# Diagonal products of chunk pairs in one run, and the first chunks' skip term through the decay matrix

## The chip, the cores and the metric

The kernel runs on one core of a Trainium2 chip. The metric is the device time of one launch in microseconds (us), the median of several runs. The core has a matrix engine (TensorE, PE in the profile, with its weight loads as PEld), a vector engine (VectorE, DVE), a scalar engine (ScalarE, ACT), a general engine (GpSimd, POOL) and an engine that mostly issues transfers (SyncE, SP). Each engine runs its own instructions in the order in which they stand; between engines semaphores order the work.

## The reference, cut to what matters

One layer of a diffusion backbone on 512 latent tokens and 256 context tokens, width 1024, all in 32-bit floats: a combined input projection feeds a bidirectional state-space mixer (SSD) and a windowed attention; both are gated, merged and projected; a convolutional feed-forward block follows. The change lies in the SSD branch, which has 32 heads of 64 columns in 4 groups of 8 heads, and works in chunks of 128 tokens. Per direction it computes, with `cs` the running sum of the log decay within a chunk:

```python
decay_to_end = jnp.exp(cs[..., -1:] - cs)
states = jnp.einsum('bcsgn,bgrcs,bcsgrp->bcgrpn', bc, decay_to_end, xc)
...
cb = jnp.einsum('bclgn,bcsgn->bgcls', cc, bc)
scores = cb[:, :, None] * jnp.exp(segsum(ac))
y_diag = jnp.einsum('bgrcls,bcsgrp->bclgrp', scores, xc)
y_off = jnp.einsum('bclgn,bcgrpn,bgrcl->bclgrp', cc, states[:, :-1], jnp.exp(cs))
return (y_diag + y_off)...
...
y = yf + jnp.flip(yb, axis=1)
y = y + d_skip * xs          # the skip term, one factor a head
out = rmsnorm(y * silu(z), g)
```

`y_diag` is the diagonal product: within a chunk, a 128x128 decay matrix per head times that head's 64 columns of input. Forward and backward are folded into one decay matrix E per head, so that the main diagonal, on which both directions meet, and the skip term `d_skip * xs` need a correction that is diagonal as well.

## The kernel before, in words

The projections are large matrix products with 512 result columns, each as three passes over operands that are split into a high and a low half (`gemm`, L238 high by high, L239 low by high, L241 high by low). Their weights come by DMA, are cast by ACT (L183, `whi`), and the rest is taken by DVE (L184, `wlo`). A list of small steps is run between the k-steps of such a product, so that the SSD branch is laid between projection products and never stands alone.

`ssd_steps(g)` writes the SSD branch of group g. For each of 4 chunks there is `chunk_in(c)` and `chunk_out(c)`:

- `chunk_in` loads the decays (`fb`), multiplies C and B into `cb` on PE (L1696), takes its diagonal `cbd` on DVE (L1698), and makes on POOL 8 numbers per token, `coef` (L1577, L1574): the factor that the diagonal correction and the skip term put on `xs`. ACT and DVE build the two tiles E of 4 heads each (L1719, L1722, L1723, L1726); DVE multiplies them by `cb` (L1730). For chunks 1 to 3 POOL spreads `coef` on a diagonal (`dg`, two tiles) and adds it to E (two additions).
- `chunk_out` multiplies the forward state Sf and the backward state Sb[c] by C (L1754, 4 matmuls each; a matmul of 32-bit operands leaves two records in the trace); DVE weighs both by the decays (L1756, `te`). Then come the diagonal products E·xs (L1762): 8 matmuls of 64 columns, of which two neighbours use the two halves of the array. `advance` moves the forward state on (matmul L1597 from `xw` and `Bk`; POOL multiplies the state by its decay, DVE adds, L1600). POOL adds both `te` into `y`. `late`, run some steps later, adds the diagonal product to `y` (DVE, L1779) and multiplies by the gate `zs` (POOL; for chunk 3 DVE).

For chunk 0 the skip and the correction go another way: POOL makes `dx` = `xs`·`coef`, and `late` adds it to the diagonal product in PSUM by 4 transposes on PE (L1778).

The backward states Sb[2], Sb[1] and Sb[0] come from the steps `back(3)`, `back(2)` and `back(1)`, each an `advance` of its own. In groups 0 to 2 all three are written ahead of `chunk_in(0)`; in group 3 `back(2)` and `back(1)` are written behind it.

The small PSUM tiles (`mis`) rotate through 5 banks. A scheduler sets the order of instructions on each engine by its own due times, except that POOL's instructions of this branch, made by `gp` and `gs`, keep the order in which the program writes them:

```python
def gp(*a):
    return tc.keep_in_program_order(G.tensor_tensor(*a))
```

Line numbers are those of the kernel before. Up to L1703 they hold after the change too; behind it L1719, L1722, L1723, L1726 and L1730 become L1722, L1725, L1726, L1729 and L1733; L1754, L1756, L1762 and L1779 become L1756, L1758, L1768 and L1782.

Of the kernel before, what the change touches and what calls it, by code (L numbers as in the profile page):

```python
# [9 lines left out]
F32 = mybir.dt.float32  # L10
# [3 lines left out]
ALU = mybir.AluOpType  # L14
# [4 lines left out]
P = 128  # L19
# [25 lines left out]
def tile_hybrid_layer(  # L45
# [32 lines left out]
    V, S, G, T = nc.vector, nc.scalar, nc.gpsimd, nc.tensor  # L78
# [3 lines left out]
    hpool = ctx.enter_context(tc.tile_pool(name="hpool", bufs=1))  # L82
# [13 lines left out]
    def bank(name):  # L96
        pool, w = banks_[name]
        return pool.tile([P, 512 * w], F32, tag=name, name=name)
# [11 lines left out]
    def misb():  # L110
        return bank("mis")
# [32 lines left out]
    for j, t in enumerate((wdn[0], DSUMS[1], DSUMS[2], DSUMS[5], DSUMS[4], wdn[1], wdn[3])):  # L144
        for u in range(DU):
            n = min(2, DK - 2 * u) * HC
# [99 lines left out]
    ident = cpool.tile([P, P], F32, name="ident")  # L246
# [181 lines left out]
    with tc.tile_pool(name="spool", bufs=1) as sp:  # L428
# [237 lines left out]
        for j in range(KT):  # L666
# [46 lines left out]
            x = ("hi", "lo") if j >= NU else ("hh", "hl")  # L713
# [31 lines left out]
        for n in range(2):  # L745
            for j in range(KT):
                x = ("hi", "lo") if j >= NU else ("hh", "hl")
# [668 lines left out]
    zp = zpool.enter_context(tc.tile_pool(name="zpool", bufs=1, side="right", reuse_waits="tile"))  # L1416
    bp = bpool.enter_context(tc.tile_pool(name="bpool", bufs=1, reuse_waits="tile"))
# [18 lines left out]
    def h8(a):  # L1436
        return a.rearrange("p (h d) -> p h d", h=8)

    def bc64(a):
        return a.unsqueeze(2).to_broadcast([P, 8, 64])  # L1440
# [132 lines left out]
    def gp(*a):  # L1573
        return tc.keep_in_program_order(G.tensor_tensor(*a))  # L1574
# [4 lines left out]
    def ssd_steps(g):  # L1579
        d = GR[g]  # L1580
# [84 lines left out]
        def far_in(c, g=g):  # L1665

            far = bp.tile([P, 2, 4, P], F32, tag="far", name="far", bufs=2)
            for u in range(2):
                a = bass.AP(
                    tensor=us_d.tensor, offset=us_d[c, u, 0, g].offset, ap=[[0, 64], [16 * P, 2], [1, 512]]  # L1670
                )
                dma = nc.sync.dma_start(far[64 * u : 64 * u + 64].rearrange("p r j t -> p r (j t)"), a)
                if not g and not c:
                    tc.add_manual_dep(dma.ins, M_LOADS["x", 16].ins.name, QUEUED, reason="decays behind a projection's weights")
            GR[g]["far", c] = far

        def chunk_in(c):

            if not g and not c:
                far_in(0)  # L1680
            fb = []
            for dr in range(2):
                f = bp.tile([P, 8, P], F32, tag="fb", name="fb", bufs=4)
                a = bass.AP(
                    tensor=cs_d.tensor, offset=cs_d.offset + (32 * dr + 8 * g) * L + c * P, ap=[[0, P], [L, 8], [1, P]]
                )
                dma = nc.sync.dma_start(f, a)
                if not g and not c:
                    tc.add_manual_dep(dma.ins, M_LOADS["x", 16].ins.name, QUEUED, reason="decays behind a projection's weights")
                fb.append(f)  # L1690
            d["E"] = []

            def products():
                cb = d["cb"] = misb()
                tok = slice(c * P, (c + 1) * P)
                T.matmul(cb[:, :P], d["BT"][:, tok], d["CT"][:, tok], start=True, stop=True)  # L1696
                cbd = bp.tile([P, 1], F32, tag="cbd", name="cbd", bufs=2)
                V.tensor_tensor_reduce(  # L1698
                    cb[:, P : 2 * P], cb[:, :P], ident, op0=ALU.mult, op1=ALU.add, scale=1.0, scalar=0.0, accum_out=cbd
                )  # L1700
                coef = d["coef"] = bp.tile([P, 8], F32, tag="coef", name="coef", bufs=2)
                gs(coef, TT[:, c, 8 * g : 8 * g + 8], cbd, None, ALU.mult)
                gp(coef, coef, bcs[:, 8 * g : 8 * g + 8], ALU.add)  # L1703
                d["dg"] = [diagonal(q) for q in range(2)] if c else None

            def diagonal(q):
                dg = bp.tile([P, 4, P], F32, tag="dg", name="dg", bufs=2)
                w = d["coef"][:, 4 * q : 4 * q + 4].unsqueeze(2).to_broadcast([P, 4, P])
                gp(dg, ident.unsqueeze(1).to_broadcast([P, 4, P]), w, ALU.mult)
                return dg  # L1710

            def decays():
                for q in range(2):
                    E = bp.tile([P, 4, P], F32, tag="E", name="E", bufs=3)
                    eb = misb()
                    F4 = fb[0][:, 4 * q : 4 * q + 4, :]
                    for u in range(4):
                        h = 8 * g + 4 * q + u
                        e0 = S.activation(E[:, u, :], F4[:, u, :], AF.Identity, bias=TX[:, c, 0, h : h + 1])  # L1719
                        if u == 0 and c:  # L1720
                            tc.keep_in_program_order(e0)
                        S.activation(eb[:, u * P : (u + 1) * P], fb[1][:, 4 * q + u, :], AF.Identity, bias=TX[:, c, 1, h : h + 1])  # L1722
                    V.copy_predicated(E, sel.unsqueeze(1).to_broadcast([P, 4, P]), eb.rearrange("p (h l) -> p h l", h=4))  # L1723
                    d["E"].append(E)
                for E in d["E"]:  # L1725
                    S.activation(flat(E), flat(E), AF.Exp)  # L1726

            def weighed():
                for q, E in enumerate(d["E"]):  # L1729
                    V.tensor_tensor(E, E, d["cb"][:, :P].unsqueeze(1).to_broadcast([P, 4, P]), ALU.mult)  # L1730
                    if c:
                        gp(E, E, d["dg"][q], ALU.add)

            if g in BY_BLOCKS and not c:
                decays()
                BETWEEN[1:2] = [lambda f=BETWEEN[1]: (f(), products(), weighed())]
            else:
                products()
                decays()
                weighed()  # L1740
            if g and c > 1:
                square()
            if g < 3 and c == 3:
                far_in(0, g + 1)

        def chunk_out(c):
            xs, E, far = d["xs"], d["E"], d.pop(("far", c))
            tok = slice(c * P, (c + 1) * P)
            parts = []
            for dr, s in ((0, d["Sf"]), (1, d["Sb"][c])):  # L1750
                ps = misb()
                for ct in range(4):
                    z = slice(ct * P, (ct + 1) * P)
                    T.matmul(ps[:, z], s[:, z], d["CT"][:, tok], start=True, stop=True)  # L1754
                t = tmp("te")
                V.tensor_tensor(t, ps, flat(far[:, dr]), ALU.mult)  # L1756
                parts.append(t)

            yd = misb()
            for h in range(8):  # L1760
                o = yd[64 * (h % 2) : 64 * (h % 2) + 64, (h // 2) * P : (h // 2 + 1) * P]
                T.matmul(o, xs[:, c, h * 64 : (h + 1) * 64], E[h // 4][:, h % 4, :], start=h < 2, stop=c > 0 and h > 5)  # L1762
            dx = None
            if not c:
                dx = zp.tile([P, 512], F32, tag="th", name="dx", bufs=1)
                gp(h8(dx), h8(xs[:, c, :]), bc64(d["coef"]), ALU.mult)
            if c < 3:
                d["Sf"] = advance(d["Sf"], 0, c, weigh_in(0, c))  # L1768
            y = bp.tile([P, 512], F32, tag="tf", name="y", bufs=1)
            gp(y, parts[0], parts[1], ALU.add)  # L1770

            def late():

                if c < 3:
                    far_in(c + 1)
                for ct in range(0 if c else 4):
                    z = slice(ct * P, (ct + 1) * P)
                    tc.keep_in_program_order(T.matmul(yd[:, z], dx[:, z], ident, start=False, stop=ct == 3, is_transpose=True))  # L1778
                tc.keep_in_program_order(V.tensor_tensor(y, yd, y, ALU.add))  # L1779
                z = d["zt"][:, :, tok]  # L1780
                x = y.rearrange("p (a t) -> p a t", a=4)
                if c == 3:  # L1782
                    V.tensor_tensor(z, x, z, ALU.mult)
                else:
                    gp(z, x, z, ALU.mult)
                if g and c in (0, 3):
                    square()

            assert not BETWEEN
            if g < 3:  # L1790
                BETWEEN.extend([lambda: None] * 4 + [lambda: (late(), turn(1)), turn])
            else:
                BETWEEN.extend([lambda: None] * 2 + [late])
# [116 lines left out]
    q2 = hpool.tile([P, L], F32, name="q2")  # L1910
# [535 lines left out]
```

## Time and profile before

| | |
|---|---|
| median of 3 runs | 1215.3 us (1214.98 to 1215.76) |
| the profiled execution's own time | 1215.35 us |
| its span in the trace | 1213.6 us, TensorE clock granted 0.999 |
| busy | PE 1203.6 us, PEld 1005.6, DVE 918.6, ACT 684.4, POOL 263.8 |
| the SSD stage with its projections, 429 to 712 us of the span | PE 282.65 us busy of 283.00 |

The span is 1.75 us shorter than the execution's time; the rest lies around it. A PE record of the trace covers a matmul from its start to its end, and neighbours overlap, so what a matmul costs is the step from its start to the start of the next, not its length. PE is busy nearly throughout, so a row of PE starts is a clock for the whole kernel: what makes PE start later makes the kernel end later, if nothing behind it absorbs it.

### The profile page before, as it was taken

To read this page: it belongs to the slowest core of one execution; us is meant where nothing else is said; L and a number is where in the kernel's file an instruction comes from. 1 tells how busy PE (TensorE), PEld (TensorE's weight loads), DVE (VectorE), ACT (ScalarE), POOL (GpSimd) and SP (SyncE) were. 2 spreads that over 40 slices of the span, in tenths; PEclk is the share of its full clock that TensorE was granted. 3 is DMA by queue.
4 is the path that set the end of the run, shared out by engine and by line. 5 is a ranking of instruction groups with operands and counts; after the bars stand their busy time and mean duration, and the time that the engine had idled before them with its cause. 6 is when DMAs were issued, how large, how long until landed. Compare 5 with 4: busy or idle time off the path is not lost.

```text
span 1213.6 us, 17847 instructions
## 1 busy us (share of the span) xinstructions
PE 1203.6 (99%) x6429; PEld 1005.6 (83%) x6429; DVE 918.6 (76%) x1476; ACT 684.4 (56%) x1269; POOL 263.8 (22%) x274
## 2 busy tenths in 40 slices
PE   9999999999999999999999999999999999999998
PEld 6798888888878878788787887888988888888886
DVE  4857887888565588788887978677677767668787
ACT  4557887778543467476575664223544343436654
POOL 0000121100102546264382762000200100110021
PEclk9999999999999999999999999999999999999999
DMA  9655889844747737566477668687266634437662
GB/s 367 253 148 185 161 229 271 170 133 139 170 140 240 228 113 199 157 162 192 145 178 264 176 228 265 221 251 242 50 163 148 195 117 138 130 107 226 213 185 97
DMA packets 129417, 224.30 MB, mean 185 GB/s; under 512 B 27336, under 2 KB 70640, under 8 KB 129328
## 3 DMA queue, kind: packets, MB, share of 16 engines
q1 hardware_dynamic: 115248, 195.61, 52.0%
q0 software_dynamic: 13792, 27.27, 10.1%
q8 instruction: 51, 0.84, 0.3%
q14 instruction: 38, 0.31, 0.1%
q10 hardware_dynamic: 288, 0.27, 0.1%
HBM read 196.17 MB, written 45.02 MB: 199 GB/s over the span
## 4 chain that ended last, share of the span: by engine, by line
PE 90%; DMA 3%; DVE 2%; POOL 2%; issue 1%; ACT 1%; SPq 0%; DVEq 0%; POOLq 0%; ACTq 0%
PE acc L241 18%; PE acc L238 18%; PE acc L239 18%; PE score L979 3%; PE po L1028 3%; PE pt L1015 2%; PE mis L582 2%; PE mis L1754 2%; PE mis L1597 2%; PE mis L2304 2%; PE mis L2302 2%; PE mis L2303 2%; DMA xs_d<-xb 1%; PE acc L2304 1%; PE acc L2302 1%
## 5 line engine op out<-in xcount | busy, mean ns | idle before, releaser
L184 DVE TENSOR_TENSOR wlo<-wraw,whi 128x1024 fp32r<-128x1024 f32 (+1 forms) x115 | 148.3, 1289 | 89.2 <-ACT whi L183 88.3
L183 ACT CAST whi<-wraw 128x1024 fp32r<-128x1024 f32 (+1 forms) x115 | 120.2, 1046 | 154.2 <-PE acc L239 103.4
L238 PE MATMUL acc<-hlh,whi 128*128 128x512 f32 x472 | 192.8, 409 | 0.0
L241 PE MATMUL acc<-hlh,wlo 128*128 128x512 f32 x472 | 185.6, 393 | 0.0
L239 PE MATMUL acc<-hll,whi 128*128 128x512 f32 x472 | 185.0, 392 | 0.0
L238 PE MATMUL acc<-mh,whi 128*128 128x512 f32 x368 | 143.3, 389 | 0.0
L239 PE MATMUL acc<-ml,whi 128*128 128x512 f32 x368 | 143.2, 389 | 0.0
L241 PE MATMUL acc<-mh,wlo 128*128 128x512 f32 x368 | 143.2, 389 | 0.0
L241 PEld LDWEIGHTS acc<-hlh,wlo 128*128 128x128 f32 x472 | 88.6, 188 | 19.9 <-issue 0.5
L238 PEld LDWEIGHTS acc<-hlh,whi 128*128 128x128 f32 x472 | 88.8, 188 | 17.6 <-issue 2.8
L239 PEld LDWEIGHTS acc<-hll,whi 128*128 128x128 f32 x472 | 88.9, 188 | 17.4 <-issue 2.2
L238 PEld LDWEIGHTS acc<-mh,whi 128*128 128x128 f32 x368 | 69.1, 188 | 14.4
L241 PEld LDWEIGHTS acc<-mh,wlo 128*128 128x128 f32 x368 | 69.1, 188 | 14.3
L239 PEld LDWEIGHTS acc<-ml,whi 128*128 128x128 f32 x368 | 69.1, 188 | 14.2
L164 POOL DMA_DIRECT2D dsum<-wdn x24 | 25.3, 1118 | 194.3 <-DVE wlo L1112 183.7
L988 DVE CUSTOM_DVE_ANT_0 p<-score,winm,nsink 128x512 f32<-128x512 f32 (+1 forms) x64 | 51.8, 810 | 15.3 <-PE score L979 13.8
L995 ACT ACTIVATE p<-p,mneg 128x512 f32<-128x512 f32 (+1 forms) x64 | 49.7, 777 | 15.4 <-DVE mneg L988 14.9
L813 DVE SCALAR_TENSOR_TENSOR tm<-wraw,csil,tm 128x512 f32<-128x512 f32 x56 | 45.9, 819 | 13.1 <-DMA wraw<-wm 12.4
L1023 DVE TENSOR_TENSOR ptl<-pt,pth 128x512 fp32r<-128x512 f32 x72 | 47.5, 685 | 8.4 <-ACT pth L1019 7.7
L238 PE MATMUL acc<-hch,whi 128*128 128x256 f32 x176 | 53.2, 302 | 0.0
L1112 DVE TENSOR_TENSOR wlo<-wraw,whi 128x1024 fp32r<-128x1024 f32 x30 | 36.7, 1223 | 18.3 <-ACT whi L1109 18.2
L241 PE MATMUL acc<-hch,wlo 128*128 128x256 f32 x176 | 49.8, 283 | 0.0
(458 smaller groups left out, 3054.3 us busy)
## 6 DMA issues: line engine op xcount, KB each, us to landing
wraw<-wup SPq DMA_DIRECT2D x44, 512.0 KB, 4.0
dsum<-wdn POOLq DMA_DIRECT2D x24, 704.0 KB, 8.7
wraw<-wm SPq DMA_DIRECT2D x32, 512.0 KB, 4.1
fb<-cs_d SPq DMA_DIRECT2D x32, 512.0 KB, 7.5
wraw<-wx SPq DMA_DIRECT2D x24, 512.0 KB, 4.1
wm<-wm SPq DMA_DIRECT2D x16, 512.0 KB, 7.9
wraw<-wz SPq DMA_DIRECT2D x16, 512.0 KB, 4.7
far<-us_d SPq DMA_DIRECT2D x32, 256.0 KB, 5.1
```

Of the source, the lines that this page charges most:

```text
L183: F["cast"] = S.copy(hi[:, :n], r[:, :n])
L184: F["sub"] = V.tensor_tensor(lo[:, :n], r[:, :n], raw(hi[:, :n]), ALU.subtract)
L238: T.matmul(ps, wh, xh[:, k0 + k, :], start=a, stop=False)
L239: T.matmul(ps, wh, xl[:, k0 + k, :], start=False, stop=False)
L241: T.matmul(ps, wl, xh[:, k0 + k, :], start=False, stop=b)
L813: V.scalar_tensor_tensor(acc, r[:, u * 512 : u * 512 + 512], sc, acc, ALU.mult, ALU.add)
L988: V.tensor_tensor_reduce(p[:, :w], d["ps"][i][:, o0 : o0 + w], m, op0=ALU.add, op1=ALU.min, scale=1.0, scalar=nsink[:, h : h + 1], accum_o ...
L995: S.activation(p, p, AF.Exp, bias=d["mneg"][:, i : i + 1], scale=-1.0, accum_out=d["den"][:, i : i + 1])
L1023: V.tensor_tensor(d["ptl"][x], d["pt"][x], raw(d["pth"][x]), ALU.subtract)
L1112: sum_step(V.tensor_tensor(d["w"][1], d["r"], raw(d["w"][0]), ALU.subtract), 1 + (4 <= g < 12))
L2302: T.matmul(ps, h, wh, start=st, stop=False, skip_group_check=True)
L2304: T.matmul(ps, h, wl, start=False, stop=en, skip_group_check=True)
```

## The change

- Chunk 0's skip and correction term goes into the decay matrix as in the other chunks: POOL makes two `dg` and two additions to E, in place of one `dx`; the 4 transposes L1778 are gone.
- The diagonal products of chunk 0, and in groups 0 to 2 of chunk 2, are held back and run right before those of the next chunk: one run of 16 matmuls, into two PSUM banks, where there were two runs of 8. In group 3 chunks 2 and 3 keep runs of their own. Of 16 runs 9 are left.
- So that E of both chunks can live together, an odd chunk's second E tile has a buffer of another pool (`rbc4`), and a held chunk's `y` too (`q2`).
- `late` handles both chunks of a run: two additions L1782 on DVE in a row, and both gate multiplications.

```diff
@@ products
-                d["dg"] = [diagonal(q) for q in range(2)] if c else None
+                d["dg"] = [diagonal(q) for q in range(2)]
@@ decays
-                    E = bp.tile([P, 4, P], F32, tag="E", name="E", bufs=3)
+                    if c % 2 and q:
+                        E = hpool.tile([P, 4, P], F32, tag="rbc4", name="E")
+                    else:
+                        E = bp.tile([P, 4, P], F32, tag="E", name="E", bufs=3)
@@ weighed
-                    if c:
-                        gp(E, E, d["dg"][q], ALU.add)
+                    gp(E, E, d["dg"][q], ALU.add)
@@ chunk_out
-            yd = misb()
-            for h in range(8):
-                o = yd[64 * (h % 2) : 64 * (h % 2) + 64, (h // 2) * P : (h // 2 + 1) * P]
-                T.matmul(o, xs[:, c, h * 64 : (h + 1) * 64], E[h // 4][:, h % 4, :], start=h < 2, stop=c > 0 and h > 5)
-            dx = None
-            if not c:
-                dx = zp.tile([P, 512], F32, tag="th", name="dx", bufs=1)
-                gp(h8(dx), h8(xs[:, c, :]), bc64(d["coef"]), ALU.mult)
+            held = c == 0 or c == 2 and g < 3
+            d.setdefault("held", []).append((c, E))
+            done = []
+            for n, Es in [] if held else d.pop("held"):
+                yd = misb()
+                for h in range(8):
+                    o = yd[64 * (h % 2) : 64 * (h % 2) + 64, (h // 2) * P : (h // 2 + 1) * P]
+                    T.matmul(o, xs[:, n, h * 64 : (h + 1) * 64], Es[h // 4][:, h % 4, :], start=h < 2, stop=h > 5)
+                done.append((n, yd))
...
-            y = bp.tile([P, 512], F32, tag="tf", name="y", bufs=1)
+            y = hpool.tile([P, 512], F32, tag="q2", name="y") if held else bp.tile([P, 512], F32, tag="tf", name="y", bufs=1)
             gp(y, parts[0], parts[1], ALU.add)
+            d["y", c] = y
@@ late
-                for ct in range(0 if c else 4):
-                    z = slice(ct * P, (ct + 1) * P)
-                    tc.keep_in_program_order(T.matmul(yd[:, z], dx[:, z], ident, start=False, stop=ct == 3, is_transpose=True))
-                tc.keep_in_program_order(V.tensor_tensor(y, yd, y, ALU.add))
...
+                for n, yd in done:
+                    y = d.pop(("y", n))
+                    tc.keep_in_program_order(V.tensor_tensor(y, yd, y, ALU.add))
+                    z = d["zt"][:, :, n * P : (n + 1) * P]
...
```

How this moves instructions, at three places. In the rows a name is a tile of the program, out<-in, then the shape of an instruction and how many stand in a row; `-` marks rows of before, `+` rows of after. First, PE in group 0 at chunk 1, where the pair's products now run (`CT` is C, `st` a state, `xw` and `Bk` the operands of `advance`, `BT` is B):

```order
 L239 MATMUL acc<-hcl,whi 128x256
 L241 MATMUL acc<-hch,wlo 128x256
-L1754 MATMUL mis<-CT,st 128x128 x8
-L1762 MATMUL mis<-E,xs 64x128 x8
+L1756 MATMUL mis<-CT,st 128x128 x8
+L1768 MATMUL mis<-E,xs 64x128 x16
 L1597 MATMUL mis<-xw,Bk 128x512
 L1696 MATMUL mis<-CT,BT 128x128
```

The run has twice its matmuls; at chunk 0 the run L1762 is gone, and L1597 follows L1756 directly.

Second, POOL in group 3 from the first backward step on (`st<-st,eT` is the multiplication of an `advance`, the last one before `y` that of the forward state, the others those of `back(3)`, `back(2)` and `back(1)`):

```order
 L1574 TENSOR_TENSOR st<-st,eT 128x512
 L1577 TENSOR_SCALAR coef<-TT,cbd 128x8
 L1574 TENSOR_TENSOR coef<-coef,bcs 128x8
-L1574 TENSOR_TENSOR st<-st,eT 128x512 x2
-L1574 TENSOR_TENSOR dx<-xs,coef 128x512
-L1574 TENSOR_TENSOR st<-st,eT 128x512
+L1574 TENSOR_TENSOR dg<-ident,coef 128x512 x2
+L1574 TENSOR_TENSOR E<-E,dg 128x512 x2
+L1574 TENSOR_TENSOR st<-st,eT 128x512 x3
 L1574 TENSOR_TENSOR y<-te 128x512
```

The multiplications of `back(2)` and `back(1)` stood right behind `coef`; now two `dg` and two additions to E stand between. On DVE the addition L1600 of `back(2)` has moved behind the two multiplications of E by `cb`, where that of `back(1)` stood already; two `te` and a `wlo` still follow them.

Third, PE at the same place, chunk 0 of group 3:

```order
 L239 MATMUL acc<-hll,whi 128x512
 L241 MATMUL acc<-hlh,wlo 128x512
-L1754 MATMUL mis<-CT,st 128x128 x8
-L1762 MATMUL mis<-E,xs 64x128 x8
+L1756 MATMUL mis<-CT,st 128x128 x4
+L238 MATMUL acc<-hlh,whi 128x512
+L239 MATMUL acc<-hll,whi 128x512
+L241 MATMUL acc<-hlh,wlo 128x512
+L238 MATMUL acc<-hlh,whi 128x512
+L1756 MATMUL mis<-CT,st 128x128 x4
 L1597 MATMUL mis<-xw,Bk 128x512
 L1696 MATMUL mis<-CT,BT 128x128
```

The four products with the forward state stand where they stood; the four with the backward state Sb[0] have moved behind four matmuls of the projection, and the diagonal products have gone to chunk 1.

More of the change, by code (lines that the diff above doesn't have):

```diff
@@ L1775, in late @@
                     far_in(c + 1)
-                for ct in range(0 if c else 4):
-                    z = slice(ct * P, (ct + 1) * P)
[L1778 to L1785, printed above, removed]
+                for n, yd in done:
+                    y = d.pop(("y", n))
+                    tc.keep_in_program_order(V.tensor_tensor(y, yd, y, ALU.add))
+                    z = d["zt"][:, :, n * P : (n + 1) * P]
+                    x = y.rearrange("p (a t) -> p a t", a=4)
+                    if n == 3:
+                        V.tensor_tensor(z, x, z, ALU.mult)
+                    else:
+                        gp(z, x, z, ALU.mult)
                 if g and c in (0, 3):
```

## Prediction

> **What bounds the kernel now.** I read the page first (busy shares, then the chain that ended last), then PE's waits, then the SSD stage by itself.
>
> ```profile
> PE 1203.6 (99%) x6429; PEld 1005.6 (83%) x6429; DVE 918.6 (76%) x1476; ACT 684.4 (56%) x1269; POOL 263.8 (22%) x274
> PE 90%; DMA 3%; DVE 2%; POOL 2%; issue 1%; ACT 1%; SPq 0%; DVEq 0%; POOLq 0%; ACTq 0%
> PE acc L241 <- DVE wlo L184: 1.3, 1, 1.3
> sum 283.00, PE 282.65 PEld 232.03 DVE 239.01 ACT 180.74 POOL 160.53; mean PE 70.66 PEld 58.01 DVE 59.75 ACT 45.19 POOL 40.13
> ```
>
> PE carries 90% of the chain, its longest wait anywhere is 1.3 us, and in the SSD stage (429 to 712 us, the sum row over four windows, one a group) it is busy 282.65 of 283.00 us. So two things set the time here: how many steps PE issues, and whether another engine comes to be waited for, which none now is. POOL has 122 us free in this stage, DVE 44; but POOL's work is in fixed order, so where it is added matters more than how much.
>
> The sum is made against the profiled execution, 1215.35 us (the span of 1213.6 and 1.75 around it); the median of the runs, 1215.3, is the same within their spread. A change under 0.2%, 2.4 us, is about what a measurement of this kernel cannot tell from none.
>
> **What PE is spared.** The timeline of PE in group 0, chunk 0, then the last of one row's records by themselves, the transposes of group 3, and the counts by line:
>
> ```profile
> 441.93 0.50 PE L1754 MATMUL mis<-CT,st 128*128 128x128 f32 x3
> 442.35 1.09 PE L1762 MATMUL mis<-E,xs 128*64 128x128 f32 x16
> 442.84 0.39 PE L1762 MATMUL mis<-E,xs 128*64 128x128 f32 x4
> 443.38 1.12 PE L1597 MATMUL mis<-xw,Bk 128*128 128x512 f32 x2
> 681.62 0.60 PE L1778 MATMUL mis<-ident,dx 128*128 128x128 f32 x4
> 682.05 0.60 PE L821 MATMUL mis<-ident,tm 128*128 128x128 f32 x4
> L1762 PE MATMUL mis<-E,xs x256: 272/273/324, 442.4 to 709.7; 128*64 128x128 f32 x128
> L1778 PE MATMUL mis<-ident,dx x16: 270/272/273, 451.8 to 681.9; 128*128 128x128 f32 x16
> ```
>
> A record is 0.27 long, so three L1754 records in 0.50 are 0.11 apart; the last starts at 442.15 and the next step was due at 442.26. E·xs starts at 442.35, 0.09 late. Its 16 records start in pairs (four records in 0.39: two starts 0.11 apart), 8 pairs or 0.88; L1597 was due at 443.23 and starts at 443.38, 0.15 late. A run therefore costs 1.12, of which 0.24 is getting in and out. A doubled run costs 0.24 + 1.76 = 2.00 where two cost 2.24. Seven runs disappear (16 to 9): 7 × 0.24 = 1.68 us saved. Bounds: 0.24 a merge at most, and nothing if the second half, in another PSUM bank, pays the entry again; I take the whole, because L1754 changes banks in the middle of its 16 records and still takes the even step (its row below: 1.95 for 16, which is 15 × 0.11 and one length).
>
> The four transposes move the next start from 681.62 to 682.05: 0.43 a group, 4 × 0.43 = 1.72 us saved, all on PE. Together 3.40 us.
>
> [...]
>
> **What is added to POOL, and where it hits.** Per group two `dg` and two additions replace one `dx`. In groups 0 to 2 it meets idle time; in group 3 it stands ahead of `back(2)` and `back(1)`. POOL in groups 0 and 1, then POOL, DVE and PE in group 3:
>
> ```profile
> 440.72 1.04 POOL L1574 TENSOR_TENSOR dx<-xs,coef 128x512 f32<-128x512 f32 x1
> 446.90 1.29 POOL L1574 TENSOR_TENSOR y<-te 128x512 f32<-128x512 f32 x1 [3.67 <-DVE te L1756]
> 450.31 2.04 POOL L1574 TENSOR_TENSOR dg<-ident,coef 128x512 f32<-128x512 f32 x2
> 452.31 2.53 POOL L1574 TENSOR_TENSOR E<-E,dg 128x512 f32<-128x512 f32 x2
> 522.73 2.21 POOL L1574 TENSOR_TENSOR y<-te 128x512 f32<-128x512 f32 x1 [3.78 <-DVE te L1756]
> L1574 POOL TENSOR_TENSOR E<-E,dg x24: 1269/1294/1749, 452.3 to 707.9; 128x512 f32<-128x512 f32 x24
> ...
> 667.67 0.21 POOL L1574 TENSOR_TENSOR coef<-coef,bcs 128x8 f32<-128x8 f32 x1
> 667.83 1.07 POOL L1574 TENSOR_TENSOR st<-st,eT 128x512 f32<-128x512 f32 x1
> 669.70 1.06 POOL L1574 TENSOR_TENSOR st<-st,eT 128x512 f32<-128x512 f32 x1 [0.80 <-DVE st L1600]
> 669.53 1.28 DVE L1730 TENSOR_TENSOR E<-E,mis 128x512 f32<-128x512 f32 x2
> 670.79 0.69 DVE L1600 TENSOR_TENSOR st<-st,mis 128x512 f32<-128x512 f32 x1
> 673.70 1.21 DVE L184 TENSOR_TENSOR wlo<-wraw,whi 128x1024 fp32r<-128x1024 f32 x1
> 672.06 1.95 PE L1754 MATMUL mis<-CT,st 128*128 128x128 f32 x16
> 676.06 0.48 PE L238 MATMUL acc<-hlh,whi 128*128 128x512 f32 x1
> 676.38 0.39 PE L239 MATMUL acc<-hll,whi 128*128 128x512 f32 x1
> 676.61 0.40 PE L241 MATMUL acc<-hlh,wlo 128*128 128x512 f32 x1
> 686.50 0.48 PE L238 MATMUL acc<-hlh,whi 128*128 128x512 f32 x1
> ```
>
> Groups 0 to 2: the addition is 2.04 + 2.53 − 1.04 = 3.53 us. POOL sits idle 3.67 and 3.78 us before `y`, waiting for `te`, so it is hidden, with little left. Cost nothing while this cover lasts; without it, rival 2.
>
> Group 3: `coef` ends at 667.88. Two `dg` take 2.04 (669.92), two additions 2.53, to 672.45; the first needs E·`cb` of DVE, ready about 670.2, which shifts the end to about 672.7. Only now comes what before began at 667.83: POOL's state, DVE's addition, POOL's state, DVE's addition, ended at 670.79 + 0.69 = 671.48, so 3.65 us. Sb[0] is ready at about 676.2. PE asks for it earlier: the order puts four matmuls with the forward state first (eight records, 0.9, from 672.06 to 672.97), then four of the projection (0.32 and three times 0.23, to 674.0), then those with Sb[0]. PE waits 2.2 us there. Breaking into the projection costs one slow step more (676.06 to 676.38 is 0.32, the next 0.23): 0.09. I take 2.3 us. Bounds: 0, if the chain were hidden; 4.1 if all four POOL instructions take the 0.45 more that the longest addition (1749 against 1294 ns) shows. I keep 2.3, since each of its links stands in a row of this stage at its usual length.
>
> Queued behind the waiting additions on DVE are two `te` and a `wlo` (673.70 before); the projection that wants the `wlo` starts only at 686.50, so it has 10 us. On POOL `y` and chunk 1's `coef`, `dg` and additions follow some 4 us later than before; by the same links chunk 1's second E is ready within some tenths of its turn in the pair: late next, priced with rival 2. SP's queue and the DMA issues keep their work.
>
> **Smaller waits on L1597.** At chunks 0 and 2 the held run no longer stands between L1754 and L1597, so PE arrives 1.12 us sooner at what L1597 needs. The four nearest cases (a copy that frees a bank, `y` that frees one, `xw`), each beside PE's last L1754 records:
>
> ```profile
> 441.27 1.03 DVE L1585 TENSOR_TENSOR xw<-xs,TD 128x512 f32<-128x512 f32 x1
> 466.79 1.84 PE L1754 MATMUL mis<-CT,st 128*128 128x128 f32 x15
> 468.27 0.36 ACT L1549 COPY xsc<-mis 128x256 f32<-128x256 f32 x1
> 545.83 1.28 PE L1754 MATMUL mis<-CT,st 128*128 128x128 f32 x10
> 546.43 0.68 DVE L1779 TENSOR_TENSOR y<-mis,y 128x512 f32<-128x512 f32 x1
> 624.70 0.61 PE L1754 MATMUL mis<-CT,st 128*128 128x128 f32 x4
> 625.27 0.36 ACT L1549 COPY xsc<-mis 128x256 f32<-128x256 f32 x1
> ```
>
> PE is due one step (0.11) after the last start, which is a record (0.27) before the row's end: 468.47, 546.95, 625.15, and 442.26 from above. What it needs ends at 468.63, 547.11, 625.63 and 442.30. Waits: 0.16 + 0.16 + 0.48 + 0.04 = 0.84, I take 0.8 us; bounds 0 (ACT and DVE, also earlier by what PE was spared before, keep ahead) and 2 × 0.84.
>
> **The sum.** 1215.35 − 1.68 − 1.72 + 2.3 + 0.8 = 1215.05, predicted 1215.1 us.
>
> **Rivals.**
>
> 1. Faster: the wait in group 3 does not come about, say because the backward chain starts earlier against PE than I place it. Then 1215.35 − 3.4 + 0.8 = 1212.7, and 1212.0 without the small waits. For it: PE's idle time there is nothing today. Against: 4.57 us of POOL work in fixed order lie ahead of Sb[0], and `coef` hangs on a PE product that moves with PE. 0.08.
>
> 2. Slower: POOL's 3.53 us do not fit. These rows show the risk, DVE's `wlo` beside POOL and alone, and PE's first run of chunk 1:
>
> ```profile
> 442.23 2.08 DVE L184 TENSOR_TENSOR wlo<-wraw,whi 128x1024 fp32r<-128x1024 f32 x1
> 664.77 1.23 DVE L184 TENSOR_TENSOR wlo<-wraw,whi 128x1024 fp32r<-128x1024 f32 x1 [2.02 <-ACT whi L183]
> 455.45 1.09 PE L1762 MATMUL mis<-E,xs 128*64 128x128 f32 x16
> ```
>
> `wlo` took 2.08 while POOL worked and 1.23 alone: DVE and POOL hold each other up. E of chunk 1 ended at 452.31 + 2.53 = 454.84; its second tile is wanted 0.44 into the run. The pair's run starts 1.12 + 0.43 earlier and reaches chunk 1 after 0.97, so it is wanted at 455.45 + 0.44 − 0.58 = 455.31: slack 0.47, plus what the 3.67 leave (0.14) and what POOL idles later. The rival decides once chunk 0's extra work delays chunk 1 by more than about 0.6 to 1. Four `dg` and additions at up to 0.45 more are 1.8 late, so about 1 us a group: 1215.1 + 3 × 1 in groups 0 to 2, and the same again in group 3, 1218 to 1219. Against: most additions take the median. 0.15.
>
> [...]
>
> 3. The merged run saves nothing, paying 0.24 between its banks: 1215.1 + 1.7 = 1216.8. Against: L1754's even step. 0.05, no measurable change.
>
> 4. A transpose holds PE for its whole record, 0.27: 16 × 0.27 = 4.35 given back in place of 1.72, 1212.4. Against: starts 0.11 apart. 0.02.
>
> **The numbers.** Forecast 0.70 (1213.6 to 1216.5 by its own bounds near the taken values), rivals 0.08, 0.15, 0.05, 0.02. Faster by over 0.2%: rivals 1 and 4, 0.10. Slower: rival 2, 0.15. The same: 0.75. The range takes rival 1 in (1212.7) and reaches into rival 2 to 1218.0, half of it.
>
> **What would show it.** In the new profile: L1768 in 9 runs, 7 of 32 records some 2.0 long; no L1778; a PE wait of about 2.3 us at the second half of L1756 in group 3's chunk 0, released by DVE's L1600; waits of tenths at L1597; POOL busy 14 us more. Wrong would be: no wait in group 3 (rival 1), or PE waits at L1768 for POOL's additions in several groups (rival 2).

## The result, and the profile after

The changed kernel takes 1230.1 us (five runs, 1227.0 to 1231.1) against 1215.8 us before (five runs, 1215.0 to 1215.9): ratio 1.011, interval 1.010 to 1.012. Forecast was 1215.1, no measurable change, at most 1218.0. The five runs lie in two groups, two at 1227.0 and three at 1230.1 to 1231.1; the profiled execution is one of the shorter (1227.05, span 1225.3), so the 3 us more of the others stand in no trace.

The page after, its busy row, its chain, and then the waits of PE between 425 and 745 us, the longest first (total, times, longest single one):

```profile
PE 1203.2 (98%) x6413; PEld 1005.9 (82%) x6413; DVE 917.9 (75%) x1476; ACT 685.2 (56%) x1269; POOL 277.1 (23%) x286
PE 82%; DVE 6%; POOL 3%; DMA 3%; ACT 2%; issue 2%; SPq 0%; DVEq 0%; POOLq 0%; ACTq 0%
PE mis L1768 <- POOL E L1574: 3.9, 3, 2.1
PE mis L1756 <- DVE st L1600: 3.1, 1, 3.1
PE mis L1597 <- ACT xsc L1549: 2.9, 2, 1.7
PE mis L1450 <- DVE tc L1431: 1.4, 2, 0.7
PE mis L1756 <- ACT xsc L1549: 1.2, 1, 1.2
PE mis L1616 <- DVE xw L1585: 0.9, 1, 0.9
PE mis L1696 <- DVE te L1758: 0.8, 1, 0.8
PE mis L1756 <- ACT xs L1549: 0.6, 1, 0.6
```

PE's share of the chain falls from 90% to 82%. Busy time hardly shows the change (POOL has 13 us more, the other engines less than 1 either way); the list of waits shows it, where before the stage had only 0.4 us, at its first instruction. In the list `xs` and `xsc` are ACT's copies, out of PSUM, of the x of the next group, `tc` is what PE transposes for them, and `te` is a product with a state, weighed by DVE.

The step of PE at a pair's run, and what PE waits for in group 3, with POOL and DVE ahead of it:

```profile
691.38 1.99 PE L1768 MATMUL mis<-E,xs 128*64 128x128 f32 x32
693.30 1.13 PE L1597 MATMUL mis<-xw,Bk 128*128 128x512 f32 x2
...
673.26 2.49 POOL L1574 TENSOR_TENSOR dg<-ident,coef 128x512 f32<-128x512 f32 x2
675.71 2.98 POOL L1574 TENSOR_TENSOR E<-E,dg 128x512 f32<-128x512 f32 x2
681.59 0.69 DVE L1600 TENSOR_TENSOR st<-st,mis 128x512 f32<-128x512 f32 x1 [1.17 <-POOL st L1574]
682.43 1.13 PE L1756 MATMUL mis<-CT,st 128*128 128x128 f32 x8 [3.08 <-DVE st L1600]
718.99 0.66 PE L1768 MATMUL mis<-E,xs 128*64 128x128 f32 x8 [2.10 <-POOL E L1574]
721.19 0.66 PE L1768 MATMUL mis<-E,xs 128*64 128x128 f32 x8 [1.55 <-POOL E L1574]
```

The doubled run moves the next start by 1.92 us: the saving came. So did the wait for Sb[0], at 3.08 us in place of 2.2 (the forecast's 2.3 has 0.09 for a slower step in it). The last two rows are chunk 3 of group 3, where nothing had been forecast.

Where PE falls behind is read by comparing the start of one instruction that both kernels have, C·B of a chunk (L1696), here that of group 3's chunk 3, before and after:

```profile
701.35 0.38 PE L1696 MATMUL mis<-CT,BT 128*128 128x128 f32 x2
709.24 0.39 PE L1696 MATMUL mis<-CT,BT 128*128 128x128 f32 x2
```

It starts 7.89 us later. The same difference at the first chunk of each group, for the kernels of the experiments too (names as in the next section; us later than in the kernel before):

| L1696 at | before | after | g3_old | g3_new | before_hold | before_62 | g3_old_62 |
|---|---|---|---|---|---|---|---|
| group 0, chunk 0 | 437.74 | -0.35 | -0.24 | -0.63 | +1.13 | -0.03 | +0.61 |
| group 1, chunk 0 | 512.38 | +2.24 | +2.41 | -0.65 | +1.66 | -0.03 | +0.99 |
| group 2, chunk 0 | 591.02 | +4.22 | +6.06 | -0.67 | +2.94 | -0.16 | +1.32 |
| group 3, chunk 0 | 664.58 | +5.31 | +7.18 | -0.24 | +3.99 | -0.17 | +1.42 |
| group 3, chunk 3 | 701.35 | +7.89 | +7.17 | +3.96 | +5.00 | -0.17 | +1.41 |

Groups 0 to 2 should each have gained 0.91 us (two merges and four transposes); in the changed kernel they fall back by 2.6, 2.0 and 1.1.

**The clock.** Stretches of the trace with PE's busy time and the granted clock (the third number from the end of a row): all of the changed kernel, first behind the waits at 719 and 721, then between 549 and 553 us.

```profile
722.00:726.00 4.00, 4.00 (x12) 3.10 (x11) 0.97 (x2) 3.60 (x6) 3.92 (x4) 0.57 0.21 80
549.00:551.00 2.00, 1.23 (x9) 1.19 (x10) 2.00 (x5) 1.18 (x3) 1.09 (x1) 1.00 0.68 143
551.00:553.00 2.00, 2.00 (x10) 1.35 (x8) 2.00 (x5) 1.42 (x4) 2.00 (x3) 1.00 0.05 13
```

At a clock of 0.57 four microseconds do the work of 2.3: by this estimate 1.7 us are lost behind the wait, a price that the forecast did not have. In that trace a step of the projection is 0.43 us long there (from 722.88 to 723.31) and 0.23 at full clock (from 726.00 to 726.23).

The traces also record each change of the granted clock. In that of the changed kernel the stretch at half clock runs from 722.20 to 725.61 us, 3.41 us; those at full clock ahead of it and behind it last 716.80 and 498.35 us, 210.0 and 146.0 times as long, and in the kernel before the one at full clock lasts 1208.32 us, 354.0 times as long. (Each of the two traces ends in a shorter stretch at half clock, 3.34 and 3.26 us.) Half clock from 550.08 to 553.5 us in g3_old and from 676.82 to 680.2 in g3_new is one such length, from 444.4 to 451.2 in skip_only two. So the traces are counted here in windows of 3.41 us, which lie differently against the program in each execution: one begins at 548.12 us in the changed kernel and at 546.66 in g3_old. PE's idle time within some windows around the waits that are discussed here and in the experiments:

| run | window, us | PE idle in it | clock of the next window |
|---|---|---|---|
| after | 544.71 to 548.12 | 0.62 | 1.00 |
| after | 548.12 to 551.53 | 1.23 | 1.00 |
| g3_old | 546.66 to 550.08 | 1.87 | 0.50 |
| after | 677.83 to 681.24 | 1.90 | 1.00 |
| after | 681.24 to 684.65 | 1.19 | 1.00 |
| g3_new | 673.40 to 676.82 | 3.03 | 0.50 |
| after | 718.79 to 722.20 | 1.74 | 0.50 |

The windows with 1.74, 1.87 and 3.03 us of idle time are followed by half clock and those with 0.62 to 1.23 are not; but neither is that with 1.90, nor the one ahead of the last row (715.38 to 718.79, 1.91), so a window's idle time does not settle it alone.

**The ledger of the profiled execution**, against the span before: saved -3.4; waits in groups 0 to 2 +7.2; Sb[0] +3.1; chunk 3 of group 3 +3.65; lowered clock +1.7; the slower step back into the projection +0.1; the wait ahead of the stage +0.5; and -1.3, since a wait of PE for `wlo` behind the stage (1.3 us before) is gone. Sum +11.55; measured 1225.3 - 1213.6 = +11.7. That it closes so well is partly luck. It leaves out that PE came 0.9 us sooner through the kernel's first 11 us in this execution (the matmul at 10.59 us before starts at 9.69). And start against start PE loses 13.7 us in the stage (from -0.35 at 438 us to 13.32 late at 712 us, where the matmul at 712.13 before starts at 725.45), while the terms of the stage give 12.4. A wait costs more than its idle time: that begins where the last record ends, 0.16 us (0.27 less 0.11) behind the moment at which the next step was due, and the stage has eleven waits.

### The profile page after: what moved, and what is told of

Same layout as the page of the kernel before. It is cut to its first block, busy times and chain, and to the rows that moved or that the text cites. A ratio compares the mean times of both kernels' runs of the same rounds, so it can differ in the third digit from the quotient of the medians.

```text
span 1225.3 us, 17814 instructions
## 1 busy us (share of the span) xinstructions
PE 1203.2 (98%) x6413; PEld 1005.9 (82%) x6413; DVE 917.9 (75%) x1476; ACT 685.2 (56%) x1269; POOL 277.1 (23%) x286
## 4 chain that ended last, share of the span: by engine, by line
PE 82%; DVE 6%; POOL 3%; DMA 3%; ACT 2%; issue 2%; SPq 0%; DVEq 0%; POOLq 0%; ACTq 0%
PE acc L241 17%; PE acc L238 17%; PE acc L239 16%; PE score L979 3%; PE po L1028 3%; PE pt L1015 2%; PE mis L582 2%; PE mis L2306 2%; PE mis L2305 2%; PE mis L2307 2%; DMA xs_d<-xb 2%; PE acc L2306 1%; PE acc L2305 1%; PE acc L2307 1%; PE acc L1098 1%
## 5 line engine op out<-in xcount | busy, mean ns | idle before, releaser
L241 PEld LDWEIGHTS acc<-mh,wlo 128*128 128x128 f32 x368 | 69.1, 188 | 14.4
L813 DVE SCALAR_TENSOR_TENSOR tm<-wraw,csil,tm 128x512 f32<-128x512 f32 x56 | 43.0, 768 | 14.1 <-DMA wraw<-wm 13.2
L1725 ACT ACTIVATE mis<-fb,TX 128x128 f32<-128x128 f32 x128 | 41.7, 357 | 14.9 <-DVE te L1758 7.0
```

The lines of the kernel that those rows point to most:

```text
L241: T.matmul(ps, wl, xh[:, k0 + k, :], start=False, stop=b)
L813: V.scalar_tensor_tensor(acc, r[:, u * 512 : u * 512 + 512], sc, acc, ALU.mult, ALU.add)
```

## The experiments

Twelve kernels, each timed in five rounds against the kernel before on the same chip (its medians 1215.1 to 1215.5). Rows carry the line numbers of the run's own kernel: L1756, L1757 are products with a state, L1768 to L1779 diagonal products.

**skip_only: no pairing.**

```diff
-            held = c == 0 or c == 2 and g < 3
+            held = False
```

> The skip term goes into the decay matrix as in the changed kernel, but every chunk keeps a run of its own for E·xs (16 runs). Banks theory (a pair's two PSUM banks, held until late, leave ACT, DVE and PE waiting for banks): those waits go, 1.7 us are saved by the transposes, only the wait for Sb[0] in group 3 stays (about 3 us), so 1215.5 - 1.7 + 3.1 = 1217 us. Rival, POOL's load (dg and additions, and DVE held up beside them) makes the loss: near 1225 us.

Measured 1231.3 us, ratio 1.013 (1.011 to 1.014). The banks' waits went, as said, but the time rose over both forecasts. PE at chunk 0 of group 0, and the clock behind that wait:

```profile
445.35 2.35 PE L1768 MATMUL mis<-E,xs 128*64 128x128 f32 x16 [3.02 <-POOL E L1574]
447.00:451.00 4.00, 4.00 (x15) 2.44 (x12) 1.20 (x2) 2.08 (x8) 1.76 (x2) 0.50 0.62 131
```

Without the hold chunk 0's run needs E at once, and POOL's `dg` and additions are late for it: 7.2 us in 7 waits for E, 3.2 for Sb[0], and three stretches of 6.8 us at half clock. So the hold hides the skip term's work; the forecast had costed the two parts as independent.

**pair_only: chunk 0's skip term stays on `dx` and transposes.**

```diff
-                d["dg"] = [diagonal(q) for q in range(2)]
+                d["dg"] = [diagonal(q) for q in range(2)] if c else None
...
+                    for ct in range(0 if n else 4):
...
+                        tc.keep_in_program_order(T.matmul(yd[:, z], d["dx"][:, z], ident, start=False, stop=ct == 3, is_transpose=True))
```

> Runs are paired as in the changed kernel, but chunk 0's skip term stays on dx and four transposes a group. Banks theory, with the two gate multiplications in a row as a second cause in group 3: the waits for ACT's copies (4.7 us in the changed kernel) and for POOL's additions at group 3's chunk 3 (3.6 us) stay, the wait for Sb[0] goes: 1215.5 - 1.7 + 8 to 10 = 1222 to 1224 us. Rival, POOL's load: 1214 us.

Measured 1238.8 us, ratio 1.019 (1.018 to 1.021): far over both numbers. POOL's added load is not in it (POOL 261.8 us busy), so it is not needed for a loss. The rest is waits of 0.5 to 1.8 us of many kinds in all groups and one of 5.4 us at group 3 with half clock around it (the row's 16 records take 3.75 us, those at 690.74 took 1.95):

```profile
712.74 3.75 PE L1757 MATMUL mis<-CT,st 128*128 128x128 f32 x16 [5.40 <-ACT whi L183]
```

It is not a clean test of pairing from group 2 on. In the program `dx` and `sq`, the squares that ACT makes for the norm, share one buffer, and `dx` now lives until the pair's transposes. ACT's `sq` of group 2 starts when a transpose (L1788) lets it, and POOL, whose order is fixed, waits for `sq` 27.0 us in two places (0.6 us in the changed kernel):

```profile
624.62 0.63 ACT L1570 ACTIVATE sq<-zs 128x512 f32<-128x512 f32 x1 [0.21 <-PE mis L1788]
625.33 1.30 POOL L1571 TENSOR_TENSOR ssq<-ssq,sq 128x512 f32<-128x512 f32 x1 [12.10 <-ACT sq L1570]
708.85 2.01 POOL L1571 TENSOR_TENSOR ssq<-ssq,sq 128x512 f32<-128x512 f32 x1 [14.91 <-ACT sq L1570]
```

From the first chunk of group 2 to that of group 3 PE falls back by 6.8 us there, and by 11.0 from there to chunk 3; the changed kernel by 1.1 and 2.6. How much of that is the shared buffer no run shows. In groups 0 and 1 PE falls back by 2.0 and 2.1 us, as in the changed kernel (2.6 and 2.0): there pairing alone makes a loss of the same size.

**before_hold: one more bank taken in the kernel before.**

```diff
+            if c == 1 or c == 3 and g < 3:
+                hold = misb()
+                T.matmul(hold[:, :8], ident, bcs[:, :8], start=True, stop=True)
...
+                    tc.keep_in_program_order(V.tensor_copy(holds, hold[:, :8]))
```

> The kernel before, with one more PSUM bank taken at the runs of chunks 1 and 3 (not 3 of group 3) by a small matmul and held until late reads 8 columns of it. Banks theory: waits of ACT for banks appear as in the changed kernel, 4 to 6 us, plus 7 small matmuls at some 0.25 us: 1221 us. Rival: only the small matmuls and copies, 1217 us.

Measured 1219.3 us, ratio 1.0033 (1.0020 to 1.0046), between the two theories. From group 0's chunk 0 to group 3's chunk 3 PE falls back by 3.9 us (table), of which seven small matmuls, at two steps of about 0.11 each, are 1.5. A held bank alone costs about 2.4 us here, not 4 to 6.

**back_first: in group 3 the backward states ahead of chunk 0's `dg`.**

```diff
+                elif "skip" in d:
+                    d.pop("skip")()      # dg and additions, issued at the end of back(1)
```

> The changed kernel, but in group 3 chunk 0's dg and additions are issued on POOL behind the states of back(2) and back(1). The wait of PE for Sb[0] (3.1 us) goes: 3 us below the changed kernel, 1224 to 1227 us. If the later wait of 3.6 us at group 3's chunk 3 were the same lateness carried on, it would go too: 1220 to 1223 us; if it comes from the two gate multiplications ahead of chunk 2's state, it stays.

Measured 1225.8 us, ratio 1.0084 (1.0070 to 1.0098). The wait for Sb[0] is gone; half of it comes back 10 us later, where the pair wants chunk 1's E, and the one at chunk 3 is untouched:

```profile
691.08 0.66 PE L1779 MATMUL mis<-E,xs 128*64 128x128 f32 x8 [1.54 <-POOL E L1574]
717.36 0.66 PE L1779 MATMUL mis<-E,xs 128*64 128x128 f32 x8 [2.10 <-POOL E L1574]
```

**g3_old and g3_new: the change cut in two at group 3.** g3_old has groups 0 to 2 changed and group 3 as before; g3_new is its complement.

```diff
+            held = g < 3 and c in (0, 2)     # g3_old; dx and transposes for g == 3
+            held = g == 3 and c == 0         # g3_new; dx and transposes for g < 3
```

> The changed kernel in groups 0 to 2, but group 3 as before (dx, transposes, four runs of its own). Theory: group 3's losses (3.1 us for Sb[0], 3.6 us at chunk 3, some 1.7 us of lowered clock) go, those of groups 0 to 2 stay: 1215.5 + 5 to 6 = 1221 us, and no stretch of lowered clock. Rival, the waits of groups 0 to 2 carry on into group 3: over 1224 us.

> Groups 0 to 2 as before, group 3 as in the changed kernel: the complement of the run with group 3 as before. Theory: the wait for Sb[0] (3.1 us) and that for POOL's additions at chunk 3 (3.6 us) are group 3's own, plus 0 to 3 us of lowered clock, less 0.7 us saved: 1215.3 + 6 to 9 = 1221 to 1224 us, and the two parts (this and the other's 7.9 us) add up to the changed kernel's 12 to 15 us. Rival, group 3 suffers from lateness carried over from groups 0 to 2: under 1218.5 us (only Sb[0]).

Measured 1223.1 us (1.0065, 1.0053 to 1.0078) and 1222.0 us (1.0064, 1.0051 to 1.0077). By the medians the parts, 8.0 and 6.7 us, add up to 14.7, the changed kernel's 14.4; by the ratios they are 7.9 and 7.8 against 13.5, so they add up within some 2 us. The loss has two homes, and group 3 does not inherit its own: in g3_new the waits are there with PE on time at its start. g3_old's forecast of an undisturbed clock failed:

```profile
547.60 1.13 PE L1757 MATMUL mis<-CT,st 128*128 128x128 f32 x8 [0.65 <-ACT xs L1549]
549.95 1.99 PE L1757 MATMUL mis<-CT,st 128*128 128x128 f32 x8 [1.22 <-ACT xsc L1549]
551.00:553.00 2.00, 2.00 (x7) 1.41 (x7) 2.00 (x5) 1.25 (x4) 2.00 (x3) 0.50 0.10 27
```

In the changed kernel the same two waits (0.62 and 1.23) left the clock at 1.00 (rows above); here it fell to 0.50, and group 1's chunk 3 starts 4.3 us late in place of 2.5. The mirror image is Sb[0]: 3.08 us at full clock there, and in g3_new

```profile
676.88 2.05 PE L1757 MATMUL mis<-CT,st 128*128 128x128 f32 x8 [3.10 <-DVE st L1600]
678.00:680.00 2.00, 2.00 (x7) 1.40 (x6) 1.16 (x2) 1.85 (x7) 0.26 (x1) 0.50 0.21 43
```

So here the length of a wait did not decide alone whether the clock fell. The table of windows above shows where the runs differ: g3_old's two waits lie in one window (1.87 us idle), the changed kernel's in two (0.62 and 1.23); the wait for Sb[0] is split there (1.90 and 1.19) and whole in g3_new (3.03).

**g3_new_zs: only one gate multiplication ahead of chunk 2's state.**

```diff
+                    elif g == 3 and n == 0:
+                        d["zs0"] = lambda z=z, x=x: gp(z, x, z, ALU.mult)   # issued in the next late
```

> The same, but the gate multiplication of chunk 0 of group 3 is issued on POOL one chunk later, so that one and not two stand ahead of chunk 2's state. If the two in a row cause the wait at chunk 3: that wait falls from 3.6 us by 1.3 to 2 us, and 2 to 4 us are won with the clock. If chunk 3's additions are late for DVE's or ACT's sake: no change.

Measured 1222.0 us, as without it. The trace shows why: the wait at chunk 3 fell from 0.88 + 1.55 to 1.26 us, by 1.2 where 1.3 to 2 had been forecast, but what was won was waited out behind the stage, at the next product's `wlo`. Nothing could be won with the clock: the stretch at half clock lies behind the wait for Sb[0] in both runs. g3_new, then g3_new_zs:

```profile
742.15 0.50 PE L241 MATMUL acc<-yh,wlo 128*128 128x512 f32 x1 [0.28 <-DVE wlo L184]
```

```profile
714.88 0.66 PE L1770 MATMUL mis<-E,xs 128*64 128x128 f32 x8 [1.26 <-POOL E L1574]
742.07 0.50 PE L241 MATMUL acc<-yh,wlo 128*128 128x512 f32 x1 [1.27 <-DVE wlo L184]
```

The two multiplications in a row are part of the cause of that wait, but about 1 us of it costs nothing.

**before_62, after_62, g3_old_62: six small banks, two for the projections.**

```diff
-    psum_pools(mis=(5, 1), acc=(3, 1))
+    psum_pools(mis=(6, 1), acc=(2, 1))
```

> Control: the kernel before, with six of the small PSUM banks and two for the projections in this stage, where it has five and three. If the third projection bank is not needed: 1215.5 us; if it is, slower by some us, which is then the base for the next runs.

> The changed kernel with six small PSUM banks and two for the projections. Banks theory: ACT no longer waits for the forward state's addition to free a bank in groups 0 to 2, and the waits of PE for ACT's copies there (4.7 us) go: 5 to 6 us less against the six-bank kernel before than the changed kernel had against the five-bank one, so +6 to +9 us over that control. Rival, contention of DVE and POOL delays ACT's and DVE's chains anyway: the distance stays 12 to 15 us.

> Both: groups 0 to 2 changed, group 3 as before, six small banks. If banks are what is lost in groups 0 to 2, three groups save 0.91 us each and nothing is lost: 2 to 3 us under the six-bank kernel before, about 1213 us. Rival: groups 0 to 2 still lose, 1217 us or more.

Measured 1231.1 us (1.014), 1240.2 us (1.020), 1236.0 us (1.017). As times these are spoilt: the control loses 16 us, nearly all of it behind the stage, most of it from where PE waits for a projection bank, with half clock after it (a projection step is 0.43 us at 731.90 and 0.23 at 734.97):

```profile
730.46 0.79 PE L238 MATMUL acc<-yh,yh 128*128 128x512 f32 x1 [7.45 <-ACT tb L778]
```

Inside the stage the control costs nothing (-0.17 us at group 3's chunk 3), so the lag there can be compared. Groups 0 to 2 changed make PE 7.4 us later with five banks (g3_old, -0.24 to +7.17, of which 1.7 is half clock) and 0.8 us with six (g3_old_62, +0.61 to +1.41); PE's waits in them fall from 7.3 to 3.3 us. That is the main evidence for banks. It is not the whole: 2.7 us were to be saved there, so six banks still leave about 3.5 us of loss. Against the control after_62 is 9.1 us longer (forecast 6 to 9, rival 12 to 15) and g3_old_62 4.9 us longer, where 2 to 3 us less had been forecast; in the stage g3_old_62 is 1.6 us behind the control, the rest comes behind it.

**g3_old_62r and g3_old_62re: five and three again behind the stage; in the second the held chunk is also added to `y` right behind the run.**

> Groups 0 to 2 changed, group 3 as before, six small PSUM banks and two for the projections in the SSD stage only, five and three again behind it. If behind the stage nothing waits for a projection bank any more: the stage's lag of 0.8 us alone, 1216 us. If the wait of 8.8 us there belongs to work that begins inside the stage: it stays, 1230 us or more.

> The same, and the held chunk's product is added to y right behind the pair's run and not with the other chunk's, which frees one of its two banks early. If what is left of the losses in groups 0 to 2 (waits of 0.4 to 1.1 us for ACT's copies and for DVE's tc) comes from the two additions in a row: 1 to 2 us below the run without it. If not: the same.

Measured 1219.3 us (1.0029, 1.0017 to 1.0042) and 1219.8 us (1.0033, 1.0021 to 1.0045). The projections' wait of 8.8 us is gone, and with it most of the loss; the early addition made no difference to the time that can be told. In the stage it did: the two waits for `tc` at group ends, 1.2 and 1.1 us in g3_old_62r, are three of 0.3 in g3_old_62re, and from group 0's chunk 0 to group 3's chunk 3 PE falls back by 2.0 us in the first and gains 0.6 in the second (L1696, against the kernel before). So with six banks and the early addition groups 0 to 2 come out ahead in the one trace; it is lost elsewhere. Neither run beats the kernel before: with two projection banks PE waits 2.2 and 2.8 us for `ta` of the convolution ahead of the stage (between 396 and 408 us), and in both it waits 1.8 and 2.1 us for `wlo` behind it, with half clock after that (steps of 0.43 us, from 741.21 and from 737.94, in place of 0.23). No tried version with the change is as fast as the kernel without it.

## Why the prediction was wrong

- **What PE is spared: right.** The merged run took 1.92 us from its start to the next; the forecast's 2.00 counts 0.09 ahead of the start, so 1.91 for the same stretch. No transposes are left: 3.4 us saved. Rivals 3 and 4 are out.
- **Groups 0 to 2, POOL's 3.53 us hidden: right**, by the hold: one wait of 0.24 us for E there. skip_only shows the price without the hold.
- **Rival 2, POOL late for chunk 1's E in every group: not in groups 0 to 2**, where its extra work was hidden as said; in group 3 chunk 1's E comes late only once the wait for Sb[0] is taken away (1.54 us in back_first).
- **The wait for Sb[0]: right in kind, 3.1 us for 2.2.** Each link had been taken at its usual length; two `dg` took 2.49 for 2.04 and two additions 2.98 for 2.53, while DVE weighed `xw` beside them. That is 0.9 us; the bound of 4.1 covered it.
- **"Smaller waits on L1597", 0.8 us: the step that failed first. Its place was taken by 7.2 us of waits in groups 0 to 2.** PE's early arrival was counted, but ACT's copies were left at their old time, and banks were looked at one instruction at a time. A pair fills two of five banks from its run until `late`, where one was filled. Group 0's chunk 2, changed kernel:

```profile
461.89 1.25 ACT L1725 ACTIVATE mis<-fb,TX 128x128 f32<-128x128 f32 x4 [0.97 <-DVE st L1600]
470.35 0.36 ACT L1549 COPY xsc<-mis 128x256 f32<-128x256 f32 x1
470.77 1.13 PE L1597 MATMUL mis<-xw,Bk 128*128 128x512 f32 x2 [1.72 <-ACT xsc L1549]
```

  ACT now waits until the forward state's addition frees a bank for the decays, the copy `xsc` behind it comes at 470.35 (468.27 before, with PE 0.32 us behind at that chunk's start), and L1597 wants the bank that the copy frees. The waits in groups 0 to 2 came to 7.2 us, 4.7 of them for ACT's copies. Banks are not the whole of it: with six, in g3_old_62, `xsc` still came at 469.93; L1597 no longer needed its bank, but the next small product did:

```profile
470.35 0.49 PE L1696 MATMUL mis<-CT,BT 128*128 128x128 f32 x2 [1.04 <-ACT xsc L1549]
```

  A held bank in the old order costs 2.4 us only (before_hold). Fewer free banks together with a PE that comes 1.12 us earlier for one would fit both; PE's early arrival was not tested by itself, so that half is argued.
- **"Late next, priced with rival 2": the place was wrong.** Chunk 1's E in group 3 was the worry; chunk 3's came late, by 3.65 us. The change moves a gate multiplication from chunk 1 to chunk 2 on POOL, ahead of `st`, and that was not followed to chunk 3. About 1.2 us of it is shown by g3_new_zs. POOL's rows give the rest, before and then after:

```profile
694.24 3.01 POOL L1574 TENSOR_TENSOR E<-E,dg 128x512 f32<-128x512 f32 x2 [1.76 <-DVE E L1730]
699.49 2.26 POOL L1574 TENSOR_TENSOR zs<-y,zs 128x512 f32<-128x512 f32 x1
706.66 2.51 POOL L1574 TENSOR_TENSOR E<-E,dg 128x512 f32<-128x512 f32 x2
...
704.53 2.52 POOL L1574 TENSOR_TENSOR E<-E,dg 128x512 f32<-128x512 f32 x2 [3.21 <-DVE E L1733]
709.22 3.53 POOL L1574 TENSOR_TENSOR zs<-y,zs 128x512 f32<-128x512 f32 x2
717.67 3.47 POOL L1574 TENSOR_TENSOR E<-E,dg 128x512 f32<-128x512 f32 x2
```

  Counted from the C·B of its chunk (L1696), chunk 3's E is done 7.8 us later before and 11.9 after, 4.1 us more. Of these 2.4 come from chunk 2's E, which DVE hands over late, 1.3 from the second gate multiplication and 1.0 from chunk 3's additions, which run beside a `wlo`; other rows give 0.6 back. DVE is late at chunk 2 because the pair's second addition waits 1.72 us for `y` of POOL and a step of another branch 1.90 us for a transfer.
- **A wait was priced at its length: the second failure.** Stretches at about half clock followed waits in after, g3_old, g3_new, skip_only, back_first (steps of 0.43 us from 721.64 us on) and pair_only, and cost, taken as half their length of 3.41 and 6.8 us, 1.7 us in each of the first three and 3.4 per stretch in skip_only. The kernel before has none in this stage, so its trace could show no such row. Nor did a wholly idle window stand ahead of each: in after and g3_old 1.74 and 1.87 us of idle time in one window of 3.41 us, with work between the waits, went before half clock.

## What to carry to other kernels

On a kernel whose bound engine never waits, price a change by what it makes late, through to the next stage. Price a new wait above its length, since here half clock followed several, at 1.7 us for a stretch of 3.41, and look at waits that lie close together as one, as g3_old's two were. Which waits it would follow no forecast from the kernel before could know: two waits of 0.65 and 1.22 us in g3_old, in one window, cost 1.7 us more than two of 0.62 and 1.23 in the changed kernel, in two. Count buffers as well as time: merging two runs holds two results at once, and every other user of those banks is a candidate for a wait. And ask of a change with two parts whether one hides the other's cost: here the skip term alone (skip_only) lost as much as both parts together, because the hold had given POOL the time for it.

## What was not expected of the hardware

- Two short waits, 0.65 and 1.22 us in one window of 3.41 us (g3_old), were followed by a granted clock of 0.50 for the next 3.41 us; a single one of 3.08 us, split over two windows (the changed kernel), by 1.00.
- Instructions of DVE and POOL took longer beside each other than forecast. POOL's two `dg` went from 2.04 to 2.49 us and its two additions from 2.53 to 2.98 beside DVE's `xw`; the same DVE instruction took 1.58 us beside the additions and 0.68 while POOL made only `coef`; and two `wlo` took 3.99 us while POOL added to E, summed squares and multiplied by the gate (one took 1.23 with POOL idle, at 664.77 us before). DVE's rows in group 3 of the changed kernel:

```profile
672.03 0.68 DVE L1585 TENSOR_TENSOR xw<-xs,TD 128x512 f32<-128x512 f32 x1
675.96 1.58 DVE L1585 TENSOR_TENSOR xw<-xs,TD 128x512 f32<-128x512 f32 x1
706.35 3.99 DVE L184 TENSOR_TENSOR wlo<-wraw,whi 128x1024 fp32r<-128x1024 f32 x2 [1.40 <-ACT whi L183]
```
